# Whole differences and seventh weight sums on GpSimd, in a seven-product hybrid decoder step

## The chip, the cores and the metric

One core of one Trainium2 chip. The metric is the device time of one execution in microseconds; the time before is the median of three runs. The engines are named as in the profile: PE (TensorE, matmuls), DVE (VectorE), ACT (ScalarE), POOL (GpSimd) and SP (SyncE, which only issues transfers here).

## The reference, cut to what matters

One layer of a decoder over 512 prompt rows and 8 sample rows, in float32. With the residual additions:

```python
proj = rmsnorm(x) @ w_in          # (520, 2048) @ (2048, 6160)
# short gated convolution on 1024 channels, gated linear attention on 1024
out = concat([ya, yb]) @ w_out    # (520, 2048) @ (2048, 2048)
x = x + out
u, v = split(rmsnorm(x) @ w_up)   # (520, 2048) @ (2048, 11264)
h = silu(causal_dwconv(u) + b) * v
x = x + h @ w_down                # (520, 5632) @ (5632, 2048)
y = rmsnorm(x)
```

The tensors that matter here are the activations of `w_out` and `w_up` and the weights of all four projections.

## The kernel before

Activations lie transposed, channels on 128 partitions and the 512 + 8 = 520 tokens along the free axis (`T` = 520, a half `HT` = 260).

**Split numbers.** Every float32 operand of a matmul is split into a high part (rounded by ACT to the matmul's own type, `hi`, line 123 for activations, line 1381 for weights) and a low part (what is left, `lo`, a subtraction with two operands in SBUF, line 124 and line 1385). A product is three passes: high by high, low by high, high by low. `split` (line 120) has the subtraction on DVE; `split_by_dma` has ACT write the negated high part and lets a transfer on POOL's queue add the source to it.

**Seven products.** Big projections are computed two-by-two blocked with seven products instead of eight (the Winograd form of Strassen's method). A *group* is seven products in the order `ORDER = (1, 5, 6, 2, 7, 3, 4)`, 24 matmuls each. Four weight blocks of 128x1024 make seven: three are loaded as they are, and four are sums. Sums 5, 6 and 3 go through one tile `s`, on DVE (line 1326). The seventh, `raw[2, 1] + raw[1, 1]`, is either one more DVE sum or, with `dma7`, an accumulating transfer of 512 KB from SBUF to SBUF on POOL's queue (line 1330). `dma7` holds for the mixer's groups ("mix"), the second half of the output projection ("wo" with `at[0] > 0`) and the up projection ("up"): 12 + 4 + 44 groups. It is called when product 5 of the group before is at hand (`j == 5`), after `prepare` has issued sum 5, which reads the same weights.

On the other side stand seven *forms* of the activations, numbered 1 to 7: three blocks as they are and four sums and differences (t1 = form 5, t2 = form 4, t3 = form 6, t4 = form 7). Each has four tiles `g` of 128x520, kept as high and low parts (`form(f, g)`; tiles named `yh`, `yl`, `bh`, `bl`, or `b` in the profile).

**Order.** The program has an order written by hand, and every engine executes its own instructions in that order. In the main loop, product `i` is followed by the finishing steps of product `i - 1`, by `prepare(i + 2)` (ACT `hi`, DVE `lo` and the next sum) and by the generators in `steps`, which yield the number of products after which their next piece is due. High and low weight tiles have three buffers each, so they are made two products ahead.

**The stages that the change touches.** While the mixer's first group runs, the forms of the mixer's input, stored earlier in `mt_d`, are loaded and split: `put` holds thirteen such splits, forms 5, 4 and 6 of tiles 1 to 3 and form 7 of tiles 0 to 3; two of form 7 go by `split_by_dma`. In the second half of the output projection, `projected(g)` runs once for each of four groups. As the sums of its output quarter `acc` are complete (accumulated by DVE from PSUM, line 1670), it stores them in `x1_d`, scales them on ACT, squares them (`square`: ACT, then an accumulating transfer on POOL's queue), makes the four differences, splits forms 1, 2, 3 and 7, and stores forms 5, 4 and 6 of groups 0 to 2 in `t_d`. Group 3 splits these too. During group 3 the nine stored tiles are loaded again (`load_sum`) and split, one after the other (`split_sums`), since the up projection's first group, which follows at once, reads all forms.

Of the kernel before, what the change touches and what calls it, by code (L numbers as in the profile page):

```python
# [9 lines left out]
F32 = mybir.dt.float32  # L10
F32R = mybir.dt.float32r
U8 = mybir.dt.uint8
AF = mybir.ActivationFunctionType
ALU = mybir.AluOpType
# [8 lines left out]
T = NP + NS  # L23
# [14 lines left out]
def trunk_kernel(  # L38
# [6 lines left out]
    nc = tc.nc  # L45
# [46 lines left out]
    def tmp():  # L92
        return tp.tile([P, T], F32, tag="t", name="t")
# [27 lines left out]
    def split(src, hi, lo, scale=None):  # L121
        if scale is None:
            nc.scalar.activation(hi, src, AF.Copy)  # L123
            nc.vector.tensor_tensor(lo, src, hi.bitcast(F32), op=ALU.subtract)  # L124
        else:
            nc.scalar.activation(hi, src, AF.Copy, scale=scale)
            nc.vector.scalar_tensor_tensor(
                lo, src, scale, hi.bitcast(F32), op0=ALU.mult, op1=ALU.subtract
            )

    def split_by_dma(src, hi, lo, again=None):
        nc.scalar.activation(hi, src, AF.Copy)
        nc.scalar.activation(lo, hi.bitcast(F32), AF.Copy, scale=-1.0)
        again = src if again is None else again
        nc.gpsimd.dma_start(lo.bitcast(F32), again, accum_op=ALU.add)

    def halves(t):
        return t[:, :HT], t[:, HT:T]
# [115 lines left out]
    def moving(pool, tag, name):  # L254

        return pool.tile([P, T + 3], F32R, tag=tag, name=name)[:, 3:]

    def pair_tiles(pool, tag):

        return [  # L260
            moving(pool, f"{tag[0]}{s}{tag[1:]}", tag[0] + s) for s in "hl"
        ]
# [17 lines left out]
    t_d = dp.tile([3, 3, P, T], F32, name="t_d")  # L280
    mt_d = dp.tile([4, 4, P, T], F32, name="mt_d")
# [55 lines left out]
    with ExitStack() as es:  # L337
# [208 lines left out]
        for k in range(KD):  # L546
            c, t = k // 4, k % 4
# [149 lines left out]

    def add(out, x, y):
        nc.vector.tensor_tensor(out, x, y, op=ALU.add)  # L699

    def sub(out, x, y):
        nc.vector.tensor_tensor(out, x, y, op=ALU.subtract)
# [42 lines left out]
    def acc_tag(n):  # L745
        return f"x{'hl'[n % 2]}{8 + n // 2}"
# [5 lines left out]
    def form(f, g):  # L752

        if f == 1:
            x = pair_tiles(bigA, f"b{g}")
        elif f in (2, 3):
            x = [
                moving(bigA, acc_tag(4 * g + q), "b2")
                for q in ((0, 3) if f == 2 else (1, 2))
            ]  # L760
        else:
            k = homes.get((f, g), {5: 0, 4: 4, 6: 8, 7: 12}[f] + g)
            x = [moving(slots[k], f"y{s}{k}", f"y{s}{k}") for s in "hl"]
        for j, q in enumerate(zip(*(halves(y) for y in x))):
            xq[f, 2 * g + j] = q
        return x
# [78 lines left out]
    with ExitStack() as mix:  # L845
# [46 lines left out]
        with ExitStack() as gl:  # L892
# [9 lines left out]
            for j in range(4):  # L902
                nc.gpsimd.affine_select(
                    out=sel, in_=sel, compare_op=ALU.not_equal, fill=1.0,
# [340 lines left out]
            for h in range(NH):  # L1245
# [21 lines left out]
                for d in range(2):  # L1267
                    ps = group(h > 0 and d == 0)
                    t = gp.tile([P, T], F32, tag="v", name="v", bufs=2)
# [16 lines left out]
    NG = KD // 4  # L1286
# [19 lines left out]
    def raw_tile(source, k):  # L1306

        w, src = wp.tile([P, 1024], F32, tag="raw", name="raw"), source(1, k)
        return w, (w.rearrange("p (k c) -> p k c", k=src.shape[1]), src)

    def weights(source, dma7, early=None):


        s = wxp.tile([P, 1024], F32, tag="s", name="s", bufs=1)
        raw = {}
        if early:
            raw = early
        else:
            raw[1, 1], first = raw_tile(source, 1)
            nc.sync.dma_start(*first)  # L1320
        raw[1, 2], rest = raw_tile(source, 2)
        if not early:
            raw.update(second_half(source))

        def plus(out, x, y):
            return lambda: nc.vector.tensor_tensor(out, x, y, op=ALU.add)  # L1326

        def dma_plus(out, x):

            return lambda: nc.gpsimd.dma_start(out, x, accum_op=ALU.add)  # L1330

        src = {
            1: raw[1, 1], 2: raw[1, 2], 3: s, 4: raw[2, 2], 5: s, 6: s, 7: raw[2, 1],
        }
        sums = {
            5: plus(s, raw[2, 2], raw[2, 1]), 6: plus(s, s, raw[1, 1]), 3: plus(s, s, raw[1, 2]),
        }
        if not dma7:
            sums[7] = plus(raw[2, 1], raw[2, 1], raw[1, 1])
        return dict(  # L1340
            src=src, sums=sums, bank={}, used=set(), rest=rest,
            seventh=dma_plus(raw[2, 1], raw[1, 1]) if dma7 else lambda: None,
        )

    groups = [("mix", (n,)) for n in range(len(MIX))]
# [345 lines left out]
    ssq, loaded = [], deque()  # L1691

    def projected(g):

        xg = {}

        def ready(q):
            a, m = acc[g, q], first_tile("wo", g, q // 2)
            kept = a
            if g == NG - 1 and q in (1, 2):  # L1700

                kept = tmp()[:, :T]
                nc.scalar.activation(kept, a, AF.Copy)
            nc.sync.dma_start(rows_of(x1_d, "wo", g, q), two(kept))
            xg[q] = tmp()[:, :T]
            for j in range(2):
                nc.scalar.activation(
                    halves(xg[q])[j], halves(a)[j], AF.Copy, scale=gffn[:, m + j : m + j + 1]
                )

        def square(q):
            if g == 0 and q in (0, 3):
                nc.scalar.activation(ssq[q % 2], acc[g, q], AF.Square)
                return
            sq = fh()
            nc.scalar.activation(sq, acc[g, q], AF.Square)
            nc.gpsimd.dma_start(ssq[q % 2], sq, accum_op=ALU.add)

        def out(f, t):

            if f == 7 or g == NG - 1:
                split(t, *form(f, g))
            else:
                nc.sync.dma_start(t_d[f - 4, g], t)

        yield 4.5
        ready(0)
        split(xg[0], *form(1, g))
        yield 5.5
        ready(3)  # L1730
        square(0)
        yield 6.5
        ready(1)
        square(3)
        yield 7
        t1, t2 = xg[0], tmp()[:, :T]
        sub(t1, xg[0], xg[1])
        minus(t2, t1, xg[3])
        yield 7.5
        ready(2)  # L1740
        out(5, t1)
        yield 8
        split(xg[2], *form(2, g))
        t4 = xg[2]
        minus(t4, t2, xg[2])
        yield 8.5
        out(4, t2)
        yield 9
        square(1)
        out(7, t4)  # L1750
        yield 10
        t3 = xg[1]
        sub(t3, xg[3], xg[1])
        yield 10.5
        square(2)
        out(6, t3)
        yield 11
        split(xg[3], *form(3, g))

    def load_sum(d, f, g, by_dma=False):  # L1760

        hi, lo = form(f, g)
        x = lo.bitcast(F32)
        nc.sync.dma_start(x, d[f - 4, g])
        if by_dma:
            return lambda: split_by_dma(x, hi, lo, d[f - 4, g])
        return lambda: split(x, hi, lo)

    def split_sums():

# [36 lines left out]
    wxr = yctx.enter_context(tc.tile_pool(name="raw2", bufs=4, side="right"))  # L1807
    wxp = yctx.enter_context(tc.tile_pool(name="sums", bufs=2, side="right"))
    early = second_half(lambda m, k: mix_source(0, m, k))
    put = [load_sum(mt_d, 5, g) for g in range(1, 4)]  # L1810
    early[1, 1], first = raw_tile(lambda m, k: mix_source(0, m, k), 1)
    nc.sync.dma_start(*first)
    ps = new_mm()
# [8 lines left out]
    assert not side  # L1822
    begin(0)
    load_rest(0)
    put += [load_sum(mt_d, 4, g) for g in range(1, 4)]
    on = [tmp()[:, :T] for _ in range(2)]
    for j, x in enumerate(on):
        nc.sync.dma_start(x, o_d[j])
    put += [load_sum(mt_d, 6, g) for g in range(1, 4)]
    y8, y9 = zpad[0][:, 2 : 2 + T], tmp()[:, :T]  # L1830
    evac(ps, y8)
    nc.scalar.activation(y8, y8, AF.Silu)
# [16 lines left out]
    bctx.close()  # L1849
    yt3 = yctx.enter_context(tc.tile_pool(name="yt3", bufs=1))  # L1850
    slots[12:] = [yt3] * 4
    put += [load_sum(mt_d, 7, g, g < 2) for g in range(4)]
    for k in range(8):
        for f, kk, b in ((1, k, 0), (2, k + 8, 0), (3, k + 8, 1)):
            xq[f, k] = [xa[kk][x][b] for x in range(2)]
# [7 lines left out]
        yield from leave(8, y8, y9)  # L1863

    def put_sums():
        for x, n in zip(put[6:], (1, 1.5, 2, 2.5, 3, 4, 4.5)):
            yield n
            x()

# [2 lines left out]
    for i, (kind, at, r) in enumerate(order):  # L1872
        j, n = i % 7, i // 7
# [41 lines left out]
        if i in (0, 2, NW, NW + 2):  # L1915

            x = xq[1, 0][0]
# [14 lines left out]
        if kind == "wo":  # L1932
            c, g = at
            if c == 0 and g == 2 and j == 0:
                load_form("wo", 1, 0)
            if c == 0 and j == 4 and g + 1 < NG:
                load_residual(g + 1)
            if c == 0 and g == 2 and j == 1:
                add_residual("wo", 0)
            if c == 0 and g == NG - 1 and j >= 1:  # L1940
                load_form("wo", 1, j)
            if c == 1 and g == NG - 1:

                for f, h in {
                    0: ((5, 0), (5, 1)), 2: ((5, 2),), 3: ((4, 0), (4, 1)), 4: ((4, 2),),
                    5: ((6, 0), (6, 1)), 6: ((6, 2),),
                }.get(j, ()):
                    loaded.append(load_sum(t_d, f, h))
        if 7 * n in (NM - 7, NU - 7):
            for x in {1: (0, 1), 2: (2, 3), 4: (4, 5), 6: (6,)}.get(j, ()):  # L1950
                load_form(groups[n + 1][0], 0, x)
# [2 lines left out]
        if kind == "down":  # L1954
            c, g = at
# [166 lines left out]
```

## Time and profile before

| what | before |
|---|---|
| median of three runs | 2129.26 us (2129.08 to 2132.24) |
| the profiled execution | 2130.32 us, of which the span from first to last instruction is 2128.6 us |
| PE busy | 2106.9 us, 99% |
| DVE busy | 1763.2 us, 83% |
| ACT busy | 1125.9 us, 53% |
| POOL busy | 421.0 us, 20% |
| granted PE clock | 0.998 |

How to read it: a row of a group has the line, engine, operation, output<-inputs by the program's names, partitions x elements of output and input, count, busy microseconds, mean nanoseconds of one, and the idle time just before with what ended it. A row of a timeline has the start and the duration in us, engine, line, operation, names, count, and in brackets the idle time before it. A row of the stages has the window, its length, then the busy time of PE, PE's weight loads, DVE, ACT and POOL (with their counts), the granted clock, the mean share of the transfer engines and GB/s; asked for one engine or line, it has that one alone. A row of waits has who waited for whom, the total in us, how often, and the longest. A row of transfers has the count, KB of one and the median us from issue to landing. Neighbouring instructions overlap a little, so a row's duration is somewhat longer than the distance from one start to the next.

### The profile page before, as it was taken

Reading aid. Unit: us, or ns where it says so; the run is one execution under the profiler, and the core shown is the slowest. Engines: PE = TensorE matmul, PEld = TensorE weight load, DVE = VectorE, ACT = ScalarE, POOL = GpSimd, SP = SyncE. Lnnn points to the kernel's source line nnn. Section 1 sums busy time; section 2 is a strip of 40 time slices with the busy share of each in tenths; the row PEclk is TensorE's granted clock in tenths of the full one; section 3 lists DMA queues with packets and bytes.
Section 4 is the critical chain, followed back from the end, with each engine's and each line's share of the span. In section 5 each row is a group of like instructions: output and inputs, shape, how many; then the busy total and the mean of one; then the engine's idle time right before and its main releaser. Section 6 shows DMA issues by size and latency. Waiting matters only on the chain.

```text
span 2128.6 us, 44249 instructions
## 1 busy us (share of the span) xinstructions
PE 2106.9 (99%) x17880; PEld 2086.8 (98%) x17880; DVE 1763.2 (83%) x2355; ACT 1125.9 (53%) x1701; POOL 421.0 (20%) x614
## 2 busy tenths in 40 slices
PE   9999999999999989999999999999999999999997
PEld 8999999999999989999999999999999999999997
DVE  6566675988888998989889989989989778888886
ACT  7454554655544776555555555555555554444445
POOL 4211221121235211211311221212212200300000
PEclk9999999999999999999999999999999999999999
DMA  8456546877789995766766766766767876994734
GB/s 258 131 169 185 164 137 186 236 199 200 192 263 278 269 287 133 196 175 171 195 177 167 196 176 167 196 176 168 195 176 193 282 227 153 274 295 131 220 110 160
DMA packets 468190, 418.37 MB, mean 197 GB/s; under 512 B 21817, under 2 KB 426569, under 8 KB 467841
## 3 DMA queue, kind: packets, MB, share of 16 engines
q1 hardware_dynamic: 424209, 289.84, 48.0%
q0 software_dynamic: 43728, 125.63, 22.6%
q8 instruction: 140, 2.29, 0.5%
q14 instruction: 65, 0.53, 0.1%
q10 hardware_dynamic: 48, 0.07, 0.0%
HBM read 300.18 MB, written 80.31 MB: 179 GB/s over the span
## 4 chain that ended last, share of the span: by engine, by line
PE 93%; DVE 2%; DMA 2%; ACT 1%; issue 1%; POOL 0%; SPq 0%; ACTq 0%; DVEq 0%; POOLq 0%
PE mm L1408 37%; PE ms L1408 15%; PE mm L146 12%; PE x L1651 9%; PE y L1651 9%; PE e L1651 4%; PE f L1651 4%; DMA raw<-in_w_in_dram 1%; DMA wgraw<-in_w_in_dram 1%; PE ms L1071 0%; DMA yl<-t_d 0%; DVE yl L124 0%; DMA t_d<-t 0%; PE ms L2012 0%; PE tp L365 0%
## 5 line engine op out<-in xcount | busy, mean ns | idle before, releaser
L1408 PE MATMUL mm<-yh,hi 128*128 128x260 f32 x1792 | 500.8, 281 | 2.5 <-DVE t L699 1.3
L1408 PE MATMUL mm<-yl,hi 128*128 128x260 f32 x1792 | 498.9, 281 | 2.5 <-DVE yl L124 2.5
L1408 PE MATMUL mm<-yh,lo 128*128 128x260 f32 x1792 | 496.4, 280 | 0.0
L1381 ACT ACTIVATE hi<-raw 128x1024 fp32r<-128x1024 f32 x336 | 354.4, 1055 | 243.4 <-issue 89.0
L1385 DVE TENSOR_TENSOR lo<-raw,hi 128x1024 fp32r<-128x1024 f32 x336 | 410.3, 1221 | 45.3 <-ACT hi L1381 41.4
L1385 DVE TENSOR_TENSOR lo<-s,hi 128x1024 fp32r<-128x1024 f32 x252 | 309.3, 1228 | 132.7 <-ACT hi L1381 132.7
L1381 ACT ACTIVATE hi<-s 128x1024 fp32r<-128x1024 f32 x252 | 266.3, 1057 | 227.5 <-PE ms L1408 97.3
L1408 PEld LDWEIGHTS mm<-yh,hi 128*128 128x128 f32 x1792 | 337.7, 188 | 3.6 <-issue 1.5
L1408 PEld LDWEIGHTS mm<-yl,hi 128*128 128x128 f32 x1792 | 335.0, 188 | 3.3 <-DVE yl L124 3.3
L1408 PEld LDWEIGHTS mm<-yh,lo 128*128 128x128 f32 x1792 | 335.9, 189 | 0.0
L1408 PE MATMUL ms<-b,hi 128*128 128x260 f32 x1408 | 264.9, 280 | 0.0
L1408 PEld LDWEIGHTS ms<-b,hi 128*128 128x128 f32 x1408 | 222.0, 188 | 0.0
L1651 PE MATMUL y<-form,hi 128*128 128x260 f32 x1120 | 211.5, 281 | 0.8 <-DVE acc L1670 0.8
L1651 PE MATMUL x<-form,hi 128*128 128x260 f32 x1120 | 211.6, 281 | 0.0
L1326 DVE TENSOR_TENSOR s<-s,raw 128x1024 f32<-128x1024 f32 x168 | 205.3, 1222 | 2.9
L1408 PE MATMUL ms<-b,lo 128*128 128x260 f32 x704 | 196.4, 280 | 0.0
L1651 PEld LDWEIGHTS y<-form,hi 128*128 128x128 f32 x1120 | 176.5, 188 | 1.2 <-ACT yh L123 1.0
L1651 PEld LDWEIGHTS x<-form,hi 128*128 128x128 f32 x1120 | 176.5, 188 | 0.2
L1651 PE MATMUL x<-form,lo 128*128 128x260 f32 x560 | 156.9, 280 | 0.0
L1651 PE MATMUL y<-form,lo 128*128 128x260 f32 x560 | 156.8, 280 | 0.0
L1408 PEld LDWEIGHTS ms<-b,lo 128*128 128x128 f32 x704 | 132.0, 187 | 0.0
L1408 PE MATMUL mm<-bh,hi 128*128 128x260 f32 x448 | 124.9, 280 | 1.0 <-DVE acc L1670 1.0
(405 smaller groups left out, 4825.2 us busy)
## 6 DMA issues: line engine op xcount, KB each, us to landing
raw<-in_w_up_dram SPq DMA_DIRECT2D x176, 512.0 KB, 4.0
raw<-in_w_down_dram SPq DMA_DIRECT2D x96, 512.0 KB, 7.3
raw<-in_w_in_dram SPq DMA_DIRECT2D x92, 512.0 KB, 4.1
form<-f_d SPq DMA_DIRECT2D x126, 260.0 KB, 6.3
raw<-raw POOLq DMA_DIRECT2D x60, 512.0 KB, 5.8
f_d<-t POOLq DMA_DIRECT2D x80, 260.0 KB, 5.5
raw<-in_w_out_dram SPq DMA_DIRECT2D x32, 512.0 KB, 12.5
form<-g_d POOLq DMA_DIRECT2D x42, 260.0 KB, 7.5
```

The lines of the kernel that those rows point to most:

```text
L146: nc.tensor.matmul(o, w, xx, start=first and i == 0, stop=last and i == 2)
L1326: return lambda: nc.vector.tensor_tensor(out, x, y, op=ALU.add)
L1381: nc.scalar.activation(his[i], src, AF.Copy)
L1385: nc.vector.tensor_tensor(los[i], src, his[i].bitcast(F32), op=ALU.subtract)
L1408: nc.tensor.matmul(st["bank"][b], w[:, k, :], x, start=b not in st["used"] and (k, j) == (0, 0), stop=(k, j) == (7, 2), skip_group_check=True,
L1651: nc.tensor.matmul(ps[:, m, :], w[:, k, m * P : (m + 1) * P], x, start=b not in st["used"] and k == 0 and j == 0, stop=k == 3 and j == 2, ...
```

## The change

- The seventh weight sum of the 60 groups with `dma7` is an addition on POOL instead of an accumulating transfer.
- `split_by_dma` becomes `split_by_pool`: ACT makes the high part, POOL subtracts.
- In `projected`, groups 0 to 2 have POOL make the low parts of forms 1, 2, 3 and 7 and the difference t3; group 3 has POOL make that of form 7. t4 has a tile of its own and no longer lies over the input of form 2, whose split comes 1.5 products later (due at 9.5 rather than 8).
- Of the nine stored tiles, four are split by POOL: forms 5, 4 and 6 of group 0 and form 5 of group 1.
- Of the mixer's thirteen splits, POOL makes five: forms 5, 4 and 6 of tile 1, form 7 of tiles 0 and 2. None goes by transfer; form 7 of tile 1 is split by DVE.

```diff
-    def split_by_dma(src, hi, lo, again=None):
+    def split_by_pool(src, hi, lo):
         nc.scalar.activation(hi, src, AF.Copy)
-        nc.scalar.activation(lo, hi.bitcast(F32), AF.Copy, scale=-1.0)
-        again = src if again is None else again
-        nc.gpsimd.dma_start(lo.bitcast(F32), again, accum_op=ALU.add)
+        nc.gpsimd.tensor_tensor(lo, src, hi.bitcast(F32), op=ALU.subtract)
...
+    def psub(out, x, y):
+        nc.gpsimd.tensor_tensor(out, x, y, op=ALU.subtract)
...
-        def dma_plus(out, x):
-            return lambda: nc.gpsimd.dma_start(out, x, accum_op=ALU.add)
+        def pool_plus(out, x):
+            return lambda: nc.gpsimd.tensor_tensor(out, out, x, op=ALU.add)
...
     def projected(g):
-        xg = {}
+        xg, final = {}, g == NG - 1
+        some = split if final else split_by_pool
...
         def out(f, t):
-            if f == 7 or g == NG - 1:
+            if f == 7:
+                split_by_pool(t, *form(f, g))
+            elif final:
                 split(t, *form(f, g))
...
-        split(xg[0], *form(1, g))
+        some(xg[0], *form(1, g))
...
         yield 8
-        split(xg[2], *form(2, g))
-        t4 = xg[2]
+        t4 = tmp()[:, :T]
         minus(t4, t2, xg[2])
...
         out(7, t4)
+        yield 9.5
+        some(xg[2], *form(2, g))
         yield 10
         t3 = xg[1]
-        sub(t3, xg[3], xg[1])
+        (sub if final else psub)(t3, xg[3], xg[1])
...
         yield 11
-        split(xg[3], *form(3, g))
+        some(xg[3], *form(3, g))
...
-    put = [load_sum(mt_d, 5, g) for g in range(1, 4)]
+    put = [load_sum(mt_d, 5, g, g == 1) for g in range(1, 4)]
...
-    put += [load_sum(mt_d, 7, g, g < 2) for g in range(4)]
+    put += [load_sum(mt_d, 7, g, g % 2 == 0) for g in range(4)]
...
-        for x, n in zip(put[6:], (1, 1.5, 2, 2.5, 3, 4, 4.5)):
+        for x, n in zip(put[6:], (1, 1.5, 2, 3, 3.5, 4, 4.5)):
...
-                    loaded.append(load_sum(t_d, f, h))
+                    loaded.append(load_sum(t_d, f, h, (f, h) in ((5, 0), (5, 1), (4, 0), (6, 0))))
```

More of the change, by code (lines that the diff above doesn't have):

```diff
@@ L1309, in raw_tile, with weights @@
         return w, (w.rearrange("p (k c) -> p k c", k=src.shape[1]), src)
-    def weights(source, dma7, early=None):
+    def weights(source, pool7, early=None):
         s = wxp.tile([P, 1024], F32, tag="s", name="s", bufs=1)
@@ L1337, in weights @@
         }
-        if not dma7:
+        if not pool7:
             sums[7] = plus(raw[2, 1], raw[2, 1], raw[1, 1])
@@ L1341, in weights @@
             src=src, sums=sums, bank={}, used=set(), rest=rest,
-            seventh=dma_plus(raw[2, 1], raw[1, 1]) if dma7 else lambda: None,
+            seventh=pool_plus(raw[2, 1], raw[1, 1]) if pool7 else lambda: None,
         )
@@ L1757, in projected, with load_sum @@
         yield 11
-        split(xg[3], *form(3, g))
-    def load_sum(d, f, g, by_dma=False):
+        some(xg[3], *form(3, g))
+    def load_sum(d, f, g, by_pool=False):
         hi, lo = form(f, g)
@@ L1764, in load_sum @@
         nc.sync.dma_start(x, d[f - 4, g])
-        if by_dma:
-            return lambda: split_by_dma(x, hi, lo, d[f - 4, g])
-        return lambda: split(x, hi, lo)
+        return lambda: (split_by_pool if by_pool else split)(x, hi, lo)
     def split_sums():
@@ L1824, in trunk_kernel @@
     load_rest(0)
-    put += [load_sum(mt_d, 4, g) for g in range(1, 4)]
+    put += [load_sum(mt_d, 4, g, g == 1) for g in range(1, 4)]
     on = [tmp()[:, :T] for _ in range(2)]
@@ L1828, in trunk_kernel @@
         nc.sync.dma_start(x, o_d[j])
-    put += [load_sum(mt_d, 6, g) for g in range(1, 4)]
+    put += [load_sum(mt_d, 6, g, g == 1) for g in range(1, 4)]
     y8, y9 = zpad[0][:, 2 : 2 + T], tmp()[:, :T]
```

## The prediction

> **What bounds the kernel now.** I read the page's busy times first, then the busy time stage by stage, then the waits, then the timelines of VectorE (DVE) and GpSimd (POOL) against TensorE (PE).
>
> ```profile
> span 2128.6 us, 44249 instructions
> PE 2106.9 (99%) x17880; PEld 2086.8 (98%) x17880; DVE 1763.2 (83%) x2355; ACT 1125.9 (53%) x1701; POOL 421.0 (20%) x614
> ```
>
> PE is busy in 99% of the span and the change leaves its matmuls alone. Time can be won only where PE waits; it is lost wherever DVE falls so far behind that PE waits more. So each stage gets two questions: does PE wait there, and how full is DVE?
>
> ```profile
> core 0: us, PE busy (x) PEld busy (x) DVE busy (x) ACT busy (x) POOL busy (x), PEclk, DMA share, GB/s
> 367.00:406.00 39.00, 37.16 (x310) 36.77 (x309) 36.95 (x51) 26.61 (x44) 8.08 (x11) 1.00 1.04 281
> 406.00:606.00 200.00, 200.00 (x1683) 200.00 (x1683) 172.10 (x220) 102.83 (x151) 42.93 (x62) 1.00 0.75 196
> 686.00:765.00 79.00, 79.00 (x661) 78.64 (x661) 73.01 (x85) 56.51 (x84) 20.58 (x27) 1.00 1.00 273
> 765.00:800.00 35.00, 29.33 (x226) 27.31 (x225) 32.28 (x42) 25.73 (x44) 5.31 (x7) 1.00 1.10 299
> 850.00:1640.00 790.00, 790.00 (x6652) 790.00 (x6651) 709.36 (x950) 432.32 (x636) 162.56 (x235) 1.00 0.70 182
> ```
>
> The rows are the mixer's first two column groups, its other groups, the second half of the output projection, the passage into the up projection, and the up projection. PE idles 1.9 us in the first row and 5.7 us in the passage. That is all there is to win: 7.6 us. In the up projection PE never idles and DVE is 90% busy; 6652 matmuls in 790 us make 0.1188 us for one and 19.95 us for a group of 168.
>
> ```profile
> PE mm L1408 <- DVE yl L124: 2.5, 4, 1.2
> ```
>
> In the passage (765 to 800 us) PE waits most for DVE's own differences (`yl`, line 124), four times: DVE is late there, more than any transfer.
>
> **What a GpSimd subtraction costs.** The trace has few, but in good places.
>
> ```profile
> 812.24 1.05 POOL L299 TENSOR_TENSOR t<-R 128x520 f32<-128x520 f32 x1 [12.78 <-ACT R L644]
> 813.37 1.31 POOL L300 TENSOR_TENSOR t<-t 128x520 f32<-128x520 f32 x1
> ...
> 816.33 2.17 POOL L302 TENSOR_TENSOR R<-R,t 128x520 f32<-128x520 f32 x1
> ```
> ```profile
> 813.44 2.33 DVE L1385 TENSOR_TENSOR lo<-s,hi 128x1024 fp32r<-128x1024 f32 x1 [1.97 <-ACT hi L1381]
> 815.93 1.39 DVE L1385 TENSOR_TENSOR lo<-raw,hi 128x1024 fp32r<-128x1024 f32 x1 [0.17 <-ACT hi L1381]
> ```
> ```profile
> L1385 DVE TENSOR_TENSOR lo<-s,hi 128x1024 fp32r<-128x1024 f32 x252 | 309.3, 1228 | 132.7 <-ACT hi L1381 132.7
> ```
>
> The DVE row at 813.44 starts 0.07 us after a POOL row and takes 2.33 us where its kind takes 1.23: it ends 1.1 us late, which is what was left of the POOL row, less 0.15. The POOL row at 816.33 starts behind a DVE row that runs to 817.32, and ends 1.2 us after that, at 818.50. So the two take turns: whoever comes second waits for the whole of the first. It holds for DVE rows with two operands in SBUF; a DVE row with one operand in PSUM runs on beside POOL:
>
> ```profile
> 152.02 2.02 POOL L296 TENSOR_TENSOR e<-bc 128x256 f32<-128x256 f32 x2 [35.61 <-DVE qm L969]
> ```
> ```profile
> 152.56 1.00 DVE L696 SCALAR_TENSOR_TENSOR yx<-yx 128x520 f32<-128x520 f32 x1
> 153.49 0.75 DVE L609 TENSOR_TENSOR k<-mm,R 128x260 f32<-128x260 f32 x2
> ```
>
> POOL works from 152.02 to 154.04; the row with two SBUF operands takes 1.00 us, the two PSUM rows (`mm`) follow at 0.37 us each, as those of `acc` and `zpad<-ms` would.
>
> Prices: 520 columns take 1.05 (one operand twice) to 1.31 us; with the 1.2 us behind 817.32 I take 1.27. No add of 1024 columns is in the trace: twice the one is 2.1 us, twice the other 2.6; I take 2.4, since a fixed part is paid once and the operands differ.
>
> [...]
>
> **Sevenths, mixer and up projection.** What goes is a transfer:
>
> ```profile
> raw<-raw POOLq DMA_DIRECT2D x60, 512.0 KB, 5.8
> ```
>
> Sixty adds of 512 KB by accumulating transfer become sixty POOL adds (12 mixer, 4 projection, 44 up). The queue issues them 0.9 us at a time; POOL now works 2.4 us, with store issues behind it. POOL is busy 163 of 790 us there, so its own time costs nothing. The sum itself comes at least 3 us sooner, and no one needs it sooner. The cost is on DVE, since the seventh may start once `s` (line 1326) has read the same weights, exactly when DVE goes on with SBUF rows. Two up groups:
>
> ```profile
> 1198.37 1.22 DVE L1385 TENSOR_TENSOR lo<-raw,hi 128x1024 fp32r<-128x1024 f32 x1
> ...
> 1200.21 0.43 DVE L1446 TENSOR_TENSOR zpad<-zpad,R 128x260 f32<-128x260 f32 x1
> 1200.89 1.23 DVE L1385 TENSOR_TENSOR lo<-s,hi 128x1024 fp32r<-128x1024 f32 x1 [0.25 <-ACT hi L1381]
> ...
> 1205.39 1.21 DVE L1385 TENSOR_TENSOR lo<-s,hi 128x1024 fp32r<-128x1024 f32 x1
> ...
> 1212.53 1.23 DVE L1385 TENSOR_TENSOR lo<-s,hi 128x1024 fp32r<-128x1024 f32 x1 [0.58 <-ACT hi L1381]
> ...
> 1224.74 1.22 DVE L1385 TENSOR_TENSOR lo<-s,hi 128x1024 fp32r<-128x1024 f32 x1
> ```
> ```profile
> 1208.11 0.28 PE L1408 MATMUL mm<-yh,hi 128*128 128x260 f32 x1
> ```
>
> POOL gets its turn when `lo` ends (1199.5) and keeps it to 1201.9; `zpad*R` waits from 1200.21 to 1201.75, which is 1.5 us, and less the 0.25 us of idle time behind it DVE is 1.2 us late. Its next tight date is the `lo` that ends at 1206.61 and is wanted by the product that starts at 1208.11: 1.5 us of lead, enough. Of the lateness 0.6 goes in the idle before 1212.53, the rest is carried into the next group, whose own seventh makes it about 2.0; there the tight `lo` ends at 1225.96 and is wanted one group (19.95 us) after 1208.11: 2.1 us of lead. So it fits, by 0.1 to 0.3 us: **0 us**, nothing below since PE does not idle, and up to 9 us (0.4 in each of 22 pairs) if a seventh holds 2.8 us.
>
> In the mixer the lead is thinner behind a "b" pair:
>
> ```profile
> 469.72 0.43 DVE L1452 TENSOR_TENSOR t<-t,zpad 128x260 f32<-128x260 f32 x1
> ...
> 474.89 1.22 DVE L1385 TENSOR_TENSOR lo<-s,hi 128x1024 fp32r<-128x1024 f32 x1
> ```
> ```profile
> 476.97 0.28 PE L1408 MATMUL mm<-yh,hi 128*128 128x260 f32 x1
> ```
>
> `zpad` waits from 469.72 to 471.5, nothing idle follows before the `lo` that ends at 476.11, 0.86 us ahead of its product: PE waits 0.9 us. Two such groups: **+2 us** (0 to 4).
>
> **The output projection's second half.** Each of the groups 0 to 2 gives POOL five DVE rows (lo of forms 1, 2, 3 and 7, and the difference t3) and a seventh. The `x1`, `t_d` stores on SP's queue keep their order; t3's store waits for POOL now. POOL's accumulating transfers of squares stand behind these rows, and ACT's squares, which have two buffers, behind those transfers; that is in the upper bound.
>
> ```profile
> 367.27 1.92 DVE L124 TENSOR_TENSOR yl<-yl,yh 128x520 fp32r<-128x520 f32 x3
> ```
> ```profile
> 731.61:751.91 20.30, 20.20 (x26) 1.00 1.05 273
> ```
>
> Three DVE differences of 520 columns take 1.92 us, 0.61 from one start to the next. The second row is DVE from `lo` of a group's second product to the same row of the next group: 20.30 us with 20.20 of work, so DVE already sets the pace (PE alone needs 19.95). The change takes out five rows of 0.61 us: 17.2 remain. POOL's turns add 5 x 1.27 + 2.4 = 8.75. What DVE can do meanwhile are six `acc` rows of 0.61, 3.7 us. If all lie beside POOL, a group takes 17.2 + 8.75 - 3.7 = 22.2; if none, 25.9. I take 22.2, as four of the six stand in the stretch in which POOL has its rows, and POOL waits at each. Three groups at +1.9 are 5.7; the first starts with weights prepared ahead, so I take **+5 us** (+2 to +14, nearly three times 25.9 - 20.3 less that lead).
>
> **The passage.** Five DVE rows go (-3.1 us); POOL makes six rows and two sevenths, 12.4 us, of which by the share above (5.0 of 8.75) 7.1 fall on DVE: +4.0. Two waits go with their rows:
>
> ```profile
> DVE b L124 <- DMA x_d<-acc: 2.4, 2, 1.6
> ```
>
> They would be worth 2.4, but the projection's lateness in `t_d` stores, and DVE's backlog, which reaches the second up group, take as much: **+4 us** (-4 to +9).
>
> **The mixer's first groups.** POOL makes five differences: four were DVE's, one an accumulating transfer. Another such transfer becomes a DVE row, so DVE has three rows fewer (-1.8 us).
>
> ```profile
> 366.12 1.23 DVE L1385 TENSOR_TENSOR lo<-raw,hi 128x1024 fp32r<-128x1024 f32 x1 [7.16 <-ACT hi L1381]
> ```
> ```profile
> 388.38 0.36 PE L1408 MATMUL mm<-yh,hi 128*128 128x260 f32 x1 [1.33 <-DVE t L699]
> ```
>
> The first seventh starts in DVE's 7.16 us of idle time and overruns it by 1.2; five differences cost about 1.0 each, as hardly any PSUM rows stand there; the second seventh 2.0. DVE is 8.2 - 1.8 = 6.4 us later, less the 39.0 - 36.95 = 2.05 us that it idles from 367 to 406: **+4.5 us** (-1.5, if nothing collides and the 1.33 us wait goes with the late transfer, to +7).
>
> **Sum.** 4.5 + 2 + 5 + 4 + 0 = 15.5 us. The profiled execution took 2130.32 us (its span and 1.7 around it), 1.06 above the median of the runs, 2129.26. 2130.3 + 15.5 gives **2146 us**, 0.8% slower. Executions shown differ by 0.15%, so 0.2% (4.3 us) is about what can be told from no change.
>
> **Rivals.** *The up projection tips* (2150 to 2180). If a seventh holds its turn 2.8 us or more, or POOL's queue delays it into a worse place, DVE needs over 19.95 us a group; 0.2 us in 44 groups are 9 us, 0.5 are 22. For it: a margin of 0.1 us. Against it: a lead of two products lets DVE rest only now and then.
> *Faster* (2121 to 2126): POOL's rows fall beside PSUM rows and idle time, DVE sheds 15 + 5 + 3 rows of 0.61, and 4 to 8 of the 7.6 us of waits go. It decides where a POOL row costs DVE under 0.6 us, the row that it takes away. For it: DVE's lateness is what PE waits for in the passage and at 388. Against it: the 1.1 us at 813.44, and 8.75 us of POOL against 3.7 of `acc`. [...]
> *Nothing to measure* (2126 to 2133.5): gain and cost cancel in the passage and the mixer, and 4 us in the projection remain at most.
>
> **Chances.** As forecast (2134 to 2162) 0.60; up projection tips 0.17; nothing 0.13; faster 0.10. Slower is 0.77. From 2130 to 2166 holds the first, two thirds of the second and half of the third.
>
> **What would show it.** DVE rows of 128x1024 at 2 to 3.6 us beside POOL rows of 1.3 and 2.4; projection groups at 22 us; PE busy less than 29.3 of 35 us in the passage; up groups still at 19.95 with a lead near 0.2. I am wrong if POOL rows leave DVE's durations alone, if a POOL row of 1024 takes 2 us or 3, or if the up groups are longer.

## The result, and the profile after

The changed kernel takes 2156.57 us (2155.97 to 2158.59, four runs); the kernel before took 2129.66 (2129.08 to 2132.24) on the same chip. The ratio is 1.0123 (95% interval 1.0108 to 1.0138): slower, as forecast, inside the range of 2130 to 2166 and 10.6 us above the 2146 named. The profiled execution took 2155.97 us, 25.65 more than that of before; the terms of the forecast add up to 15.5.

First the page of the changed kernel: the span and the busy times of the engines.

```profile
span 2154.2 us, 44272 instructions
PE 2116.0 (98%) x17880; PEld 2093.2 (97%) x17880; DVE 1862.0 (86%) x2332; ACT 1119.8 (52%) x1699; POOL 599.4 (28%) x637
```

GpSimd (POOL) took over work, yet VectorE (DVE) is busy 99 us *longer* with 23 instructions fewer: a row that waits for its turn counts as busy (5.38 us for 1.22 at 728.30, below). The stages, in the columns of the prediction's second fence:

```profile
367.00:406.00 39.00, 34.32 (x270) 33.62 (x269) 38.75 (x40) 22.85 (x38) 15.91 (x13) 0.96 0.68 200
406.00:606.00 200.00, 198.12 (x1658) 197.43 (x1658) 183.93 (x218) 100.66 (x149) 64.21 (x56) 1.00 0.59 164
686.00:765.00 79.00, 72.17 (x595) 70.95 (x594) 70.32 (x63) 45.51 (x67) 42.95 (x38) 1.00 0.78 234
765.00:800.00 35.00, 28.92 (x224) 28.14 (x222) 33.44 (x27) 23.57 (x39) 27.48 (x19) 0.95 0.93 261
850.00:1640.00 790.00, 789.38 (x6634) 788.39 (x6633) 768.34 (x953) 430.11 (x640) 246.02 (x226) 1.00 0.54 152
```

TensorE (PE) worked through 79 us of the third row before and misses 6.8 us of it now; the up projection, with two thirds of all sevenths, misses 0.6 of 790. The granted clock is below 1 in two rows; before, it was 1.00 in all five.

Where the 25.65 us lie is read from the starts of TensorE's products, group by group, against the same groups of before:

| stage (groups) | predicted us | measured us |
|---|---|---|
| mixer's first two groups | +4.5 | +4.80 |
| mixer's other ten | +2 | +3.01 |
| projection's first half (4) | not listed | +0.51 |
| projection's second half (4) | +5 | +11.47 (0.97, 3.41, 3.63, 3.46) |
| passage: first four up groups | +4 | +5.09 |
| other forty up groups | 0 | +0.67 |

Start and end give 0.1. One term is off by more than a factor of two. Two of its parts can be seen at once. VectorE and GpSimd beside each other in the second half, from the two engines' timelines of the changed kernel:

```profile
727.17 1.21 DVE L1385 TENSOR_TENSOR lo<-raw,hi 128x1024 fp32r<-128x1024 f32 x1
728.30 5.38 DVE L1327 TENSOR_TENSOR s<-s,raw 128x1024 f32<-128x1024 f32 x1
733.60 1.21 DVE L1385 TENSOR_TENSOR lo<-raw,hi 128x1024 fp32r<-128x1024 f32 x1
```
```profile
727.80 0.94 POOL L1718 DMA_DIRECT2D R<-fh  x1 [6.60 <-ACT fh L1717]
728.43 1.65 POOL L133 TENSOR_TENSOR yl<-t,yh 128x520 fp32r<-128x520 f32 x1
729.70 1.63 POOL L133 TENSOR_TENSOR b<-t,b 128x520 fp32r<-128x520 f32 x1
730.99 1.59 POOL L700 TENSOR_TENSOR t<-t 128x520 f32<-128x520 f32 x1
```

The sum `s` starts 0.13 us *ahead* of GpSimd's first row and should be first. It takes 5.38 us where its kind takes 1.22: it ran only after all three rows, 4.15 us late. And ACT's waits from 700 to 800 us of the changed kernel, beside the same in the kernel before:

```profile
ACT fh L1717 <- DMA ssq<-fh: 5.3, 2, 3.9
```
```profile
758.58 0.64 ACT L1716 ACTIVATE fh<-acc 128x520 f32<-128x520 f32 x1 [0.24 <-DMA ssq<-fh]
```

ACT waits 5.3 us (3.9 once) for a tile whose square is still being transferred; in the kernel before it waits 0.24. ACT's high parts, VectorE's low parts and the product stand behind it.

### The profile page after: what moved, and what is told of

Its sections match the earlier page's. It is cut to its first block, busy times and chain, and to the rows that moved or that the text cites. A ratio compares the mean times of both kernels' runs of the same rounds, so it can differ in the third digit from the quotient of the medians.

```text
span 2154.2 us, 44272 instructions
## 1 busy us (share of the span) xinstructions
PE 2116.0 (98%) x17880; PEld 2093.2 (97%) x17880; DVE 1862.0 (86%) x2332; ACT 1119.8 (52%) x1699; POOL 599.4 (28%) x637
## 4 chain that ended last, share of the span: by engine, by line
PE 82%; DVE 8%; issue 3%; DMA 3%; ACT 1%; SPq 1%; POOL 1%; ACTq 0%; DVEq 0%; POOLq 0%
PE mm L1408 32%; PE ms L1408 13%; PE mm L144 12%; PE y L1651 8%; PE x L1651 8%; PE e L1651 3%; PE f L1651 3%; DVE lo L1385 3%; DVE s L1327 1%; DMA raw<-in_w_out_dram 1%; DMA wgraw<-in_w_in_dram 1%; DVE yl L124 1%; PE ms L1072 0%; DMA ssq<-fh 0%; DVE acc L1670 0%
## 5 line engine op out<-in xcount | busy, mean ns | idle before, releaser
L1385 DVE TENSOR_TENSOR lo<-raw,hi 128x1024 fp32r<-128x1024 f32 x336 | 417.4, 1242 | 39.4 <-ACT hi L1381 36.2
L1385 DVE TENSOR_TENSOR lo<-s,hi 128x1024 fp32r<-128x1024 f32 x252 | 326.5, 1296 | 72.5 <-ACT hi L1381 72.5
L1330 POOL TENSOR_TENSOR raw<-raw 128x1024 f32<-128x1024 f32 x60 | 192.0, 3200 | 283.9 <-DVE s L1327 260.9
L1327 DVE TENSOR_TENSOR s<-s,raw 128x1024 f32<-128x1024 f32 x168 | 219.5, 1307 | 2.9
```

The source lines that it names most:

```text
L1330: return lambda: nc.gpsimd.tensor_tensor(out, out, x, op=ALU.add)
L1385: nc.vector.tensor_tensor(los[i], src, his[i].bitcast(F32), op=ALU.subtract)
```

## The experiments

Three theories go through them. A is the prediction's: the engines take turns, one for one. B: squares' transfers land late, so ACT waits for its square tiles. E, formed on the way: VectorE is shut out through several GpSimd rows in a row. Each ratio is against the kernel before, run in the same set. "Second half" and "passage" are sums over the groups of the table above, "held" are VectorE rows above 5 us there, "ACT" is its waits for squares' transfers, all from the profiled execution.

| kernel | us | ratio (95%) | second half | passage | held | ACT |
|---|---|---|---|---|---|---|
| changed | 2156.57 | 1.0123 (1.0108–1.0138) | +11.47 | +5.09 | 5.38 | 5.3 |
| e1 sevenths only | 2146.73 | 1.0073 (1.0056–1.0089) | +8.47 | +0.93 | none | 3.5 |
| e2 differences only | 2145.21 | 1.0067 (1.0052–1.0082) | +10.29 | +2.08 | 5.30, 7.51, 5.47 | 0 |
| e3 no square transfers | 2148.37 | 1.0078 (1.0063–1.0093) | +4.06 | +4.70 | none | none |
| e4 memsets | 2126.68 | 0.9973 (0.9963–0.9983) | −1.58 | −0.85 | none | 6.9 |
| e5 squares first | 2154.48 | 1.0110 (1.0097–1.0124) | +10.69 | +4.76 | 5.67 | 2.6 |
| e6 projection undone | 2154.39 | 1.0112 (1.0096–1.0127) | +6.54 | +7.98 | none | 4.1 |
| e7 sevenths on VectorE | 2134.50 | 1.0018 (1.0009–1.0026) | +1.61 | +1.05 | none | – |
| e8 mixer on VectorE | 2132.17 | 1.0002 (0.9993–1.0011) | +0.51 | −0.80 | none | – |
| e10 tiny transfers | 2167.21 | 1.0163 (1.0149–1.0176) | +18.70 | +6.43 | 5.02 | 16.9 |
| e12 four square tiles | 2160.17 | 1.0138 (1.0119–1.0156) | +15.95 | +8.18 | 5.38, 7.67, 7.22 | 0 |

**e1, sevenths only.** The kernel before, with `dma_plus` made an addition on GpSimd:

```diff
-            return lambda: nc.gpsimd.dma_start(out, x, accum_op=ALU.add)
+            return lambda: nc.gpsimd.tensor_tensor(out, out, x, op=ALU.add)
```

> The kernel before with one part of the change: the sixty seventh weight sums are GpSimd adds, all differences stay where they were. Theory A (GpSimd and VectorE take turns on rows with two SBUF operands): the mixer's groups 5 and 9 get 1.6 and 1.0 us longer as in the changed kernel, the up projection 1 us in all, the first pair 1 us, and in the projection's second half, where VectorE is full, each of three groups gets 1.5 to 2 us longer: +8 to +11 us, 2138 to 2141. Theory D (all the cost is in the differences, a seventh is hidden by the two products of lead): at most +3, 2130 to 2133.

**e2, differences only.** The changed kernel, with the same line turned back into the transfer.

> The changed kernel with the sixty seventh sums as accumulating transfers again: only GpSimd's differences remain. Theory A: the mixer's groups 2 to 11 and the up projection are back at the times of before; group 0 keeps about 3.5 us, the projection's second half 2 to 4 of its 11.5, the passage 3 to 5: 2138 to 2143. Theory D: 2151 to 2155, since only the mixer's and the up projection's 4 us go.

Both are dearer than theory A had them (2138 to 2141 and 2138 to 2143 us). By groups, e1 loses 14.5 us and e2 15.1 (a start later by 1.3 us in e1, ahead of the first seventh, left out); together 29.6, where the changed kernel loses 25.6. Both halves cost, the sevenths as much as the differences (against theory D), and they are not independent: e2 alone has three held rows and no wait of ACT, the whole has one held row and the wait.

**e3, no square transfers.** The changed kernel without the line that adds a square to its sum by transfer.

```diff
-            nc.gpsimd.dma_start(ssq[q % 2], sq, accum_op=ALU.add)
```

> The changed kernel without the accumulating transfers of squares in the output projection (ACT still squares; the second norm's sums are left out, so the numbers behind it are wrong). Theory B (behind GpSimd's rows these transfers come late, ACT's next square but one waits for its buffer, and hi, lo and the product behind it with ACT): the second half falls from +11.5 to about +5.5 over before, the passage loses 1 to 2 more: 2147 to 2151. Theory A alone (turns with VectorE explain all of the second half): within 1.5 us of the changed kernel, 2155 to 2158.

The second half falls to +4.06. This looked like proof of B, and was not: two things had gone at once, as the timelines of this kernel show.

```profile
750.85 2.33 DVE L1327 TENSOR_TENSOR s<-s,raw 128x1024 f32<-128x1024 f32 x1
753.11 2.34 DVE L1385 TENSOR_TENSOR lo<-raw,hi 128x1024 fp32r<-128x1024 f32 x1
```
```profile
750.65 1.45 POOL L133 TENSOR_TENSOR yl<-t,yh 128x520 fp32r<-128x520 f32 x1 [6.90 <-ACT yh L132]
752.13 2.24 POOL L133 TENSOR_TENSOR b<-t,b 128x520 fp32r<-128x520 f32 x1
754.33 2.31 POOL L700 TENSOR_TENSOR t<-t 128x520 f32<-128x520 f32 x1
```

Here the engines alternate strictly, as predicted: VectorE waits out one row and GpSimd the next, each late by 1.1 us. So +4.06 is what GpSimd's rows cost here without chains and without ACT's wait, near the +5 forecast.

**e4, memsets.** The changed kernel with three memsets in place of each GpSimd subtraction or addition: a GpSimd that is nearly as busy (the 180 memsets of the sevenths 171.5 us, where the changed kernel's sixty additions take 192.0) but reads nothing from SBUF.

> The changed kernel with three memsets of the same tile in the place of each of GpSimd's subtractions and adds: GpSimd is busy about as long (2.7 us for a seventh, 1.5 for a difference) and in the same places of its queue, but reads nothing (low parts and seventh sums are left out, the numbers are wrong). Theory A: VectorE's 128x1024 rows are back at 1.22 us, the mixer and the up projection at the times of before; what is left is B's part in the projection: 2130 to 2138. Rival C (GpSimd's results come late, or its queue holds back transfers; VectorE is not held): the times stay near the changed kernel's, 2150 to 2158.

Faster than before by 0.27%, and below A's range too; VectorE has fewer rows here than before (2332 for 2355) and is not held. So the theory named C in it falls with D, which e1 has refuted: GpSimd's time in itself cost nothing here (0.9973); with the rows that read SBUF in the same places the ratio is 1.0123. ACT's waits for squares are here too, 6.9 us, and the second half does not get longer by them (−1.58).

**e5, squares first.** The changed kernel with the squares' transfers ahead of GpSimd's rows: `square(2)` moved to 9.5, ahead of form 2's split, and

```diff
-        if j == 5 and more:
-            state[groups[n + 1]]["seventh"]()
         run_steps(i + 0.5)
+        if j == 5 and more:
+            state[groups[n + 1]]["seventh"]()
```

> The changed kernel with nothing left out, but with GpSimd's queue in another order: in the projection's groups the square of the third quarter is made before form 2's low part is given to GpSimd, and the seventh sum is given to GpSimd behind the steps of the same place instead of ahead of them. So the accumulating transfers of squares stand ahead of GpSimd's rows. Theory B (ACT waits for its square tile, because the transfer that frees it stands behind GpSimd's rows): ACT's wait of 3.9 us near 757 goes, the four groups of the projection's second half cost +4 to +6 us over before (+4.1 without those transfers, +11.5 in the changed kernel), and the time is 2148 to 2151 us. Rival (what costs is that VectorE waits through several GpSimd rows in a row, whatever the transfers do): the rows are the same and as close together, the second half stays at +9 to +12 and the time at 2154 to 2157.

The rival's numbers. ACT's wait is halved, but a held row of 5.67 us at 758.81 comes in its place.

**e6, projection undone.** The changed kernel with VectorE making the projection's five rows a group again (`some = split`, `sub` for t3, `split` for form 7).

> The changed kernel with one part undone: in the projection's second half VectorE makes the low parts of forms 1, 2, 3 and 7 and the difference t3 again; the sevenths, the mixer's and the passage's rows stay on GpSimd. If the parts add up, the mixer keeps its +8 and the passage its +5, and the second half falls from +11.5 to what the sevenths alone cost there (+5.7): 2150 to 2152 us. Rival (the passage costs only because VectorE comes late out of the projection): the passage falls to +2 or less as well, and the time is 2147 to 2149 us.

The second half falls by 4.9 us to +6.54, over the +5.7 expected, and the passage gives 2.9 back: 2154.4 us, above both forecasts. (The +5.7 is not what e1 measured for the sevenths there, +8.47.) The rival falls: the passage is dear though the projection ends earlier. That the rows in the passage make it so is likely, not shown; two spells of half clock of 3.4 us lie in it (797 and 814), where the changed kernel has one of 6.8.

**e7, sevenths on VectorE.** The kernel before, with `dma7` false everywhere: VectorE makes all sixty sums.

> The kernel before, with all sixty seventh sums made by VectorE instead of by transfer: 1.23 us more of VectorE's own work in each of the sixty groups, and no GpSimd row. Theory A (a GpSimd add shuts VectorE out for what is left of its 2.4 us, which is more than the 1.23 us that VectorE needs for the same sum): cheaper than the sevenths on GpSimd, which cost +15.8 by groups: mixer 0 to +2 instead of +4.8, second half +4 to +5 (20.2 + 1.2 = 21.4 us a group against 20.3, four times), passage +1 to +3, up projection 0 (709 + 54 of 790 us busy): 2135 to 2140 us. Rival (an engine's work that is moved off VectorE is worth its duration there even if it shuts VectorE out now and then): the same as sevenths on GpSimd or more, 2145 us and up.

The kernel of e7, mixer and up projection:

```profile
406.00:606.00 200.00, 200.00 (x1684) 200.00 (x1683) 182.76 (x230) 103.03 (x151) 33.62 (x52) 1.00 0.61 169
850.00:1640.00 790.00, 790.00 (x6652) 790.00 (x6651) 751.57 (x993) 441.52 (x642) 125.77 (x194) 1.00 0.55 155
```

Theory A holds, and its rival of 2145 us falls: 1.23 us of VectorE's own work in each group costs the mixer's last ten groups and the up projection nothing at all, where GpSimd's 2.4 us cost those ten 3.0. The second half is cheaper than A had it (+1.61 for +4 to +5). Against e1 the same sums are 0.55% cheaper. Here a GpSimd seventh is dearer *for VectorE* than doing the work itself.

**e8, mixer on VectorE.** The kernel before, with all that the change needs no GpSimd row for: the mixer's two transfers made VectorE rows at the new places, t4 in a tile of its own, form 2's split at 9.5.

> The kernel before, with the two differences of the mixer's form 7 that go by accumulating transfer made by VectorE, at the changed kernel's places in the order, and with t4 in its own tile and form 2's split 1.5 products later, as in the change; GpSimd makes no whole difference and no seventh. It is all of the change that needs no GpSimd row. If the new places are worth something by themselves (the 1.33 us that PE waits at 388 behind a late transfer), 2127 to 2129 us; if VectorE is late by the two added rows of 0.61 us, 2130 to 2131 us. In both cases the change's +25 us is GpSimd's rows.

No difference from before. The change's new order is free here (1.0002); its cost is GpSimd's rows.

**e9, chains.** The kernel before, with sixteen unneeded bursts of three GpSimd rows in the up projection, half of them behind the issue of a small transfer.

```diff
+            nc.scalar.activation(pa, h1, AF.Copy)
+            nc.gpsimd.memset(pa[:, :64], 0.5)
+            if chains[i]:
+                nc.gpsimd.dma_start(probe_d.pop(), ones[:, :1])
+            for _ in range(3):
+                nc.gpsimd.tensor_tensor(pa, l1, h1, op=ALU.subtract)
```

> The kernel before with sixteen bursts of GpSimd work that nobody waits for, one in every second group of the up projection, in eight places of the group: a copy by ACT, a memset of 64 columns that waits for it, and three subtractions of 520 columns with two SBUF operands, back to back. In eight of the sixteen, the issue of a small transfer stands between the memset and the subtractions. It asks when a VectorE row waits for one GpSimd row and when for the whole chain (5.4 us at 728 in the changed kernel, 2.3 us in the one without the squares' transfers). Theory E (rows that follow the issue of a transfer on GpSimd start before the row ahead of them has ended, and then give VectorE no turn): VectorE's weight rows beside the eight bursts with a transfer take up to 4 to 5 us, beside the eight without one at most 2.4 us. Rival (it is the moment: VectorE is shut out when it comes less than 0.2 us ahead of the first row): long and short rows lie in both kinds alike. Theory A as predicted (one for one, always): no VectorE row over 2.5 us.

No weight row above 2.34 us beside any of the sixteen (one run, 2133.65 us). One of them, behind a transfer's issue:

```profile
992.23 2.31 DVE L1387 TENSOR_TENSOR lo<-raw,hi 128x1024 fp32r<-128x1024 f32 x1 [0.34 <-ACT hi L1383]
994.56 2.23 DVE L1387 TENSOR_TENSOR lo<-s,hi 128x1024 fp32r<-128x1024 f32 x1
```

So E as worded there falls: a transfer's issue alone does not make a chain. Nor does the moment with it: at 1155.86 and 1476.71 a VectorE row starts 0.2 us ahead of a burst behind an issue, as at 728.30, and waits for one row (2.10 us in all). The burst also misses something that the real rows have: its rows write one tile, and each starts only when the one ahead has ended.

**e10, tiny transfers.** The changed kernel with 512 bytes in place of each square's 260 KB.

```diff
-            nc.gpsimd.dma_start(ssq[q % 2], sq, accum_op=ALU.add)
+            nc.gpsimd.dma_start(probe_d.pop(), sq[:, :1])
```

> The changed kernel with the squares' accumulating transfers of 260 KB cut to 512 bytes at the same places (one column of the square, stored to DRAM); the second norm's sums of squares leave out what those transfers would add, as without them. GpSimd issues a transfer ahead of its rows as in the changed kernel, and ACT's square tile is free soon. Theory B (the second half is dear because ACT waits for the square tile): +4 us in the second half as without the transfers (+4.06), 2148 to 2149 us. Theory E (a transfer's issue ahead of GpSimd's rows makes them one chain that shuts VectorE out): VectorE rows of over 5 us come back near 728 and 750, the second half is +8 to +11, and the time 2152 to 2156 us.

Dearer than both theories say. A row of 5.02 us is back at 728.63. And these transfers of 512 bytes, one column of 128 partitions to DRAM, are no sooner done (11.3 us, the median) than those of 260 KB (5.4 and 6.8 in the changed kernel). Two rows of this kernel, its transfers and ACT's waits:

```profile
probe<-fh POOLq DMA_DIRECT2D x14, 0.5 KB, 11.3
```
```profile
ACT fh L1718 <- DMA probe<-fh: 16.9, 4, 8.7
```

ACT waits for the landing here too; the worst wait, 8.7 us, stops TensorE for 6.7, with 6.8 us at half clock behind it. That a wait of ACT can cost the second half dearly is shown here. e4 has 6.9 us of such waits for nothing; that they cost only where VectorE has no slack is argued from this, not shown.

**e11, pauses of TensorE.** The kernel before, with sixteen pauses between two matmuls. It changes part of the computed output; only pauses and clock are read.

```diff
+            nc.tensor.matmul(pb[:, :P], ones, ones, start=True, stop=True)
+            for _ in range(pauses[i]):
+                nc.gpsimd.memset(ones, 1.0)
+            nc.tensor.matmul(pb[:, :P], ones, ones, start=True, stop=True)
```

> The kernel before with sixteen pauses of TensorE in the up projection, one in every second group: a matmul, then 4, 7, 10, 13, 16, 19, 22 or 26 short memsets on GpSimd, then a matmul that waits for them; every length twice. It asks which pauses are followed by a stretch of half the granted clock: in the changed kernel a pause of 2.56 us was and one of 2.59 us was not. If a length decides, pauses up to about 2.2 us are followed by none and those from 3.5 us all are, each by 3.4 or 6.8 us at 0.5, which costs up to 1.7 or 3.4 us more than the pause. If the clock drops for other reasons (what came before in a longer window), pauses of one length differ, or none is followed by a drop.

One run, 2239.07 us. Groups with a pause of 2.23, 3.02 and 3.81 us in them, in this order:

```profile
911.00:931.00 20.00, 18.04 (x153) 17.85 (x152) 14.36 (x20) 7.57 (x12) 2.33 (x8) 1.00 0.57 145
955.00:975.00 20.00, 17.25 (x133) 17.06 (x132) 12.12 (x14) 6.66 (x10) 2.95 (x11) 0.91 0.52 131
1000.00:1020.00 20.00, 16.47 (x119) 16.27 (x118) 10.41 (x13) 6.14 (x9) 3.55 (x14) 0.83 0.45 120
```

Pauses of 1.38, 1.44 and 2.23 us leave the clock alone and lengthen their group by 0.4 more than themselves. Both of 3.02 us are followed by 3.4 us at half clock (1.5 us dearer), all from 3.8 us on by 6.8 or 10.2 (the two of 3.81: 2.5 dearer).

The profiles say more than the length of a pause does. In every kernel with several spells of half clock they begin whole multiples of 3.41 us apart (376.8, 776.2 and 800.1 us in the changed kernel: 117 and 7 of them). Cut on that grid, the fourteen profiles have 37 windows at full clock between 360 and 2060 us that a spell follows. In all 37 TensorE is idle for 0.56 of the window or more; in no other window at full clock for more than 0.54. The changed kernel's pause of 2.56 us lies in one window (0.64), the one of 2.59 at 747.43 is split between two, a third of each: the one is followed by a spell and the other is not.

**e12, four square tiles.** The changed kernel with nothing else altered, so that ACT need not wait:

```diff
-            sq = fh()
+            nsq[0] += 1
+            sq = fh() if nsq[0] % 4 < 2 else zpad[nsq[0] % 2][:, 2 : 2 + T]
```

> The changed kernel with one more thing: ACT writes the squares of the projection into four tiles by turns instead of two (the other two are the mixer's convolution tiles, which are idle there). All transfers and all of GpSimd's rows stay, in their order. Theory B (the second half is dear because ACT waits until the transfer of the square before the last has landed): ACT's waits of 2.3 to 3.9 us for the transfers go, the four groups of the second half cost +4 to +5 us over before instead of +11.5, and the time is 2148 to 2150 us. Rival (the dear part is VectorE shut out through three or four GpSimd rows in a row, when its row starts less than 0.2 us ahead of the first): rows of 5 to 7.5 us remain, the second half is +8 to +12, and the time 2153 to 2157 us. If each holds half of it, +7 to +8 and 2151 to 2153 us.

ACT's waits for transfers are gone, and the second half is dearer than even the rival had it. Its two timelines, at a place where the changed kernel has no held row:

```profile
760.16 7.67 DVE L1385 TENSOR_TENSOR lo<-raw,hi 128x1024 fp32r<-128x1024 f32 x1 [0.39 <-ACT hi L1381]
767.76 0.68 DVE L1670 TENSOR_TENSOR acc<-acc,x 128x520 f32<-128x520 f32 x1
```
```profile
758.66 0.85 POOL L1719 DMA_DIRECT2D R<-fh  x1 [9.81 <-ACT zpad L1718]
759.22 1.62 POOL L133 TENSOR_TENSOR yl<-t,yh 128x520 fp32r<-128x520 f32 x1
760.50 1.60 POOL L133 TENSOR_TENSOR b<-t,b 128x520 fp32r<-128x520 f32 x1
761.78 1.58 POOL L700 TENSOR_TENSOR t<-t 128x520 f32<-128x520 f32 x1
763.04 1.15 POOL L1719 DMA_DIRECT2D ssq<-zpad  x1
763.64 1.87 POOL L133 TENSOR_TENSOR b<-t,b 128x520 fp32r<-128x520 f32 x1
764.91 1.83 POOL L133 TENSOR_TENSOR bl<-t,bh 128x520 fp32r<-128x520 f32 x1
```

One weight row waits through five GpSimd rows and an issue, 6.45 us late. The likely reason is that ACT's wait had kept GpSimd's rows off VectorE, and that without it they arrive together. So B names a real wait and not the whole cause: take it away and the dearer one shows. Some of e12's +15.95 and +8.18 is the clock: spells of 3.4 and 6.8 us begin at 769 and 790, one of 6.8 at 821.

## Why the prediction was right, and the term that was not

- *The signs and the frame.* "DVE falls so far behind that PE waits more" is what happened, in the tight stages, and e4 (0.9973), e7 (1.0018) and e8 (1.0002) confine it to GpSimd's rows that read SBUF.
- *GpSimd's prices.* 2.4 us for 1024 columns: 2.39 at the shortest; the median row takes 3.25, since most start 0.2 us into a VectorE row and wait for its end. 1.27 for 520: 1.27 and 1.29 from one start to the next at 728. Right. The fixed part that it counted once shows in the kernel before: 256 columns took 0.65 us there and 512 took 1.15 (medians, line 296).
- *Turns, one for one.* "Whoever comes second waits for the whole of the first" is right where the engines alternate (e3: 2.33 and 2.34 us for 1.22; e9: at most 2.34), in the mixer and, but for two rows, in the up projection. The row at 728.30 started first and waited through three; and two rows in the up projection of the changed kernel, at 1047.48 and 1487.13, started first and waited for a single seventh, which took 2.40 us (the shortest of the sixty took 2.39). By the starts in the profile VectorE came first in these three and waited all the same: a row's start is not yet its turn.

```profile
1047.48 3.82 DVE L1327 TENSOR_TENSOR s<-s,raw 128x1024 f32<-128x1024 f32 x1
```
```profile
1047.80 2.40 POOL L1330 TENSOR_TENSOR raw<-raw 128x1024 f32<-128x1024 f32 x1
```

- *Mixer's first groups, +4.5.* Its terms give 4.35. Measured +4.80, so close by luck, since a part has another reason: turns make TensorE pause 2.56 us at 374.38, and then 3.4 us at half clock add 1.5 (that product takes 4.70 us for 3.21).
- *Mixer, +2.* Two "b" groups, as said: +1.64 and +0.97 instead of 0.9 each.
- *Projection's second half, +5.* The term that was mis-sized: +11.47. Its working has GpSimd's rows hold VectorE once each, and e3 measures that at +4.06. What it left out are chains (4.15 us on one row) and ACT's wait (5.3), of which it put the latter "in the upper bound" of +14; a half-clock spell at 776 adds 1.5. These do not simply add, as e5 and e12 show: less of the wait gives more of the chains.
- *The passage, +4.* Measured +5.09, near by luck too: some 2.5 of it are 6.8 us at half clock behind a pause of 4.35 us (estimate, from e11's pauses with such a spell).
- *Up projection, 0.* +0.67, nearly all in three groups of forty (0.31, 0.21, 0.15); the first two are those with the rows at 1047.48 and 1487.13, 2.6 and 2.5 us late. The lead, worked out as 0.1 to 0.3 us, held in the rest; e7 shows that 1.23 us more of VectorE's own work fits too.
- *The clock* stood nowhere in the working. Three spells after pauses cost about 1.5 + 1.5 + 2.5 = 5.5 of the 25.65 us, by e11's prices (an estimate).

Still open: what decides between alternating and a chain. All rows held through three or more GpSimd rows (nine, in the changed kernel, e2, e5, e10 and e12) belong to a run that begins 0.6 us behind the issue of a square's transfer, and in it a row starts before the row ahead has ended, 1.26 to 1.30 us after its start. e3 without those issues has none; e9 with smaller issues, and rows that wait for each other, has none either. An issue ahead is not enough in the real order either: in the changed kernel the run at 759.42 stands 0.57 us behind a square's issue, and its rows and VectorE's alternate. What else it takes, the overlapping starts, the moment or both, was not separated.

No kernel here beats the one before with all of the computation in it: e8 is level, and the 7.6 us of waits that the prediction counted stay.

## What to carry to other kernels

Work given to an idle engine is not free if its rows and the busy engine's shut each other out (here the kernel got 1.2% slower): count the rows of both that would meet, not the engine's busy share, and compare with the busy engine doing the work itself (here 1.23 us of its own against waits of up to 2.6 for one GpSimd sum). Price turns as one for one only where rows of the helper stand alone; a run of them can cost its whole length at once (4.15 us for three rows at 728.30, 6.45 for five and an issue in e12). When an experiment removes a wait, look whether a second thing went with it (e3), and test the wait alone (e12) before calling it the cause.

## What the runs showed of the hardware

- A VectorE row with two SBUF operands waited through three to five GpSimd rows in nine cases (changed kernel, e2, e5, e10, e12): 5.0 to 7.7 us for work of 1.2 us. Beside GpSimd's memsets (e4) none took over 5 us, and the mean of 252 and of 336 weight rows was 1.23 and 1.22.
- Some pauses of TensorE were followed by half the granted clock for 3.4 us or a multiple of it (3.41 and 6.83 in the changed kernel, up to 10.2 in e11). Single pauses up to 2.23 us were not; those of 3.53 and 4.35 us in the changed kernel and all from 3.8 us on in e11 were. Between, both ways: 2.56 us in the changed kernel with it and 2.59 without, 3.02 in e11 with it and 3.17 in e12 without. What separates them in these traces is how much the pauses fill of a window of 3.41 us, cut on the grid of the spells' starts: 0.56 or more against at most 0.54. Several short ones in one window did it too (e11 at 789.9, where the longest was 1.53 us).
- Beside weight loads that themselves took 13 to 16 us, a transfer of 512 bytes, one column of 128 partitions, to DRAM took 11.3 us (median of 14) from issue to landing in e10, more than the 5.4 to 6.8 of the 260 KB in the changed kernel.
